# A decoder trunk's expert stage in two passes: gates scattered into a table in DRAM

## The chip, the cores and the metric

The kernel runs on one core of a Trainium2 chip. The metric is the time of one execution on the device in microseconds, the median of several. Matrix products run on TensorE, elementwise work and searches on VectorE (DVE in the profile), activations and casts on ScalarE (ACT), some elementwise work on GpSimd (POOL); SyncE (SP) issues most of the DMAs. The profile shows a matmul as PE and a weight load as PEld.

## The reference, cut to what matters

The program is a trunk of two layers on 256 tokens of width 1024. A layer is a mixing stage (a recurrence and attention side by side, one output projection, a layer norm) and then the expert stage, `_peer`. In it every token picks 128 of 16384 experts: 8 heads times 16.

```python
def _peer(x, wq, subkeys, u_tab, v_tab):
    xf = x.reshape(T, D)
    q = (xf @ wq).reshape(T, PEER_HEADS, 2, PEER_KEY_DIM)
    s = jnp.einsum('thcd,ckd->thck', q, subkeys).astype(jnp.float32)
    sv, si = lax.top_k(s, PEER_TOPK)
    cand = (sv[:, :, 0, :, None] + sv[:, :, 1, None, :]).reshape(T, PEER_HEADS, PEER_TOPK * PEER_TOPK)
    cv, ci = lax.top_k(cand, PEER_TOPK)
    ea = jnp.take_along_axis(si[:, :, 0], ci // PEER_TOPK, axis=-1)
    eb = jnp.take_along_axis(si[:, :, 1], ci % PEER_TOPK, axis=-1)
    experts = (ea * PEER_KEYS + eb).reshape(T, PEER_HEADS * PEER_TOPK)
    gate = jax.nn.softmax(cv, axis=-1).reshape(T, PEER_HEADS * PEER_TOPK).astype(x.dtype)
    ...
        act = jax.nn.gelu(jnp.einsum('cd,ced->ce', xc, u_tab[ec]))
        return jnp.einsum('ce,ced->cd', act * gc, v_tab[ec])
```

So the output of a token is a sum over its experts e of gate(e) * gelu(x . u[e]) * v[e]. Several heads of a token may pick the same expert; their gates then add up.

## The kernel before, in words

The kernel does not gather experts. It computes the dense form: for all 16384 experts and all 256 tokens the first product with gelu, multiplies it by a dense matrix G of gates (zero where an expert was not picked), and takes the second product with the whole of v. The experts are cut into 128 tiles of 128. Each tile has a first product (`u_tile`, lines 742 to 757) and a second one (`v_tile`, lines 977 to 985).

A first product is in one of two forms. In the split form (`wtile`, lines 97 to 109, and `col_mm` with `mm3`, lines 111 to 117) SyncE loads 512 KB into `raw` (four buffers), ScalarE casts it to `hi` (L104), VectorE or GpSimd subtracts to get `lo` (L105), and TensorE runs 8 x 3 matmuls (L113). In the f32 form (`raw_mm`, L140) TensorE multiplies the raw tile; the profile shows 16 records for its 8 matmuls. Tiles 14 to 33 have the f32 form, all others the split form; tiles 0 to 13 have their `lo` on GpSimd. Two tiles share a PSUM bank, and ScalarE's gelu (L752) writes a pair of them as one `act` tile of 256 KB.

A second product splits the weighted activations into W (ScalarE L963, VectorE L964), splits 512 KB of v in the same way, and runs 12 matmuls of 512 columns (L972) that sum up in four PSUM banks.

The order of a layer's expert stage is the program's text, lines 826 to 1086:
- queries and scores of the eight heads (`query`, `top`), each score row searched for its 16 largest on VectorE (`best16`, L791 to L795), the pair sums searched in the same way (`pairs`), with first products 0 to 13 behind them (lines 826 to 842);
- the choices: an exponential on ScalarE (L848), comparisons and sums in f16 on VectorE (L857 to L888), all eight heads at once;
- three transposes (L895), which give the experts' two halves and the gates by token (`eT`, `gT`);
- the one-hot stage: 32 rounds of `onehots` (lines 918 to 939), each two one-hot products on VectorE (L923, L927) for eight tokens, 16 matmuls (L934) and four copies on ScalarE (L938) into G, which fills 128 KB of every SBUF partition. Twelve f32 first products lie between the rounds;
- the dense stage (lines 1055 to 1081): first and second products alternate. The activations of the first 34 tiles, which were computed before G was there, had been written to DRAM (`kept`, issued by ScalarE) and are fetched back (`fetch`, L952); the others are used from SBUF. `w_pair` (L950) multiplies a pair by G.

Near the end of the stage parts of G are free and take weights of the next layer and the last tiles of v (`slot`, `take`, `parts`), and the last tiles are interleaved with the second layer norm by a hand-written order (`ORDER2`). The mixing stage has a hand-written order too, `ORDER`, one string of steps per layer; its steps `l0` to `l13` load w_out (`o0` to `o7`), the first queries' weights (`f0` to `f3`) and two tiles of wq (`w0`, `w1`). All these loads are on SyncE's queue, which runs in order and waits where a buffer is not free.

```python
for i in range(32):
    onehots(8 * i)
    while au < 2 * NSP and (au - 2 * NU0 + 1) * 32 <= (i + 1) * (2 * NSP - 2 * NU0):
        u_tile(au)
        au += 1
```

Of the kernel before, what the change touches and what calls it, by code (L numbers as in the profile page):

```python
# [21 lines left out]
S = 256  # L22
# [4 lines left out]
GSC = 32768.0  # L27

ORDER = ("d2 I0 c0 d4 I1 g2 d1 V3 c1 V1 V2 P V0 G3 G0 d0 G1 g0 b0 b1 g1 d3 T h0 d5 G2 q2 h1 q1 g3 kv D S q0 q3 "
# [19 lines left out]
NACT = 8  # L49
NU0 = 11  # L50
NSP = 17
# [18 lines left out]
for _name, _w in (("ident", 128), ("one", 1), ("av", 2), ("iota", 128), ("i16", 16), ("st16", 16), ("dist", 256),  # L70
                  ("ctab", 256), ("hm", 8), ("sel0", 128), ("sel1", 128)):
    CC[_name] = slice(_n, _n + _w)
    _n += _w
NCC = _n
NC0 = CC["av"].stop
# [3 lines left out]
def trunk_kernel(ctx: ExitStack, tc: tile.TileContext, x, xt, cst, lam, pvec, brow, w_in, w_lx, w_v, w_q4, lru_w,  # L79
# [162 lines left out]
    iota = cpool.tile([128, 128, 2], F16, name="iota")  # L242
# [21 lines left out]
    spill = ctx.enter_context(tc.tile_pool(name="spill", bufs=1, space=bass.MemoryType.DRAM))  # L264
    pw = {}
    nc.sync.dma_start(C, cst[:, :NC0])
    for l in range(NL):
# [3 lines left out]
        with tc.tile_pool(name="mix", bufs=1, reuse_waits="tile") as mp, \  # L271
# [7 lines left out]
            POOL.memset(onerow, 1.0)  # L279

# [377 lines left out]
            def tables():  # L658
                if l == 0:
                    softplus()  # L660
                    DVE.tensor_copy(identb, ident)
                    DVE.tensor_copy(iota, mc("iota").unsqueeze(2).to_broadcast([128, 128, 2]))
                    DVE.tensor_copy(i16[:, 0], mc("i16"))
                    DVE.tensor_copy(i16[:, 1], mc("st16"))
# [29 lines left out]
            def nsa_end(qb):  # L694
# [8 lines left out]
                         Q=qfirst, R=q_rows, I=lru_in, V=lru_conv, P=proj_v_end, d=const_load)  # L703
# [26 lines left out]
        with tc.tile_pool(name="peer", bufs=1, reuse_waits="tile") as pp:  # L730

            eT = pp.tile([128, 128, 2, 2], F16, name="eT")
            gT = pp.tile([128, 128, 2, 2], F16, name="gT")
            act = {}
            kept = {}

            ub = {}

            def act_tile():
                return pp.tile([128, 2, S], F32, name="act", bufs=NACT)  # L740

            def u_tile(a):
# [3 lines left out]
                if NPOOL <= a < 2 * NSP:  # L746
                    raw_mm(ps[:, HALF[a % 2]], rtile(u_tab[l, a], (8, 128)))
                else:
                    col_mm(ps[:, HALF[a % 2]], wtile(u_tab[l, a], (8, 128), POOL if a < NPOOL else DVE), xT)
                if a % 2:  # L750
                    at = act_tile()
                    ACT.activation(at.rearrange("p a b -> p (a b)"), ps, AF.Gelu_apprx_tanh)  # L752
                    if a // 2 < NSP:
                        kept[a - 1] = spill.tile([128, 2, S], F32, name="kept%d" % (a - 1), bufs=1)
                        ACT.dma_start(kept[a - 1], at)
                    else:
                        act[a - 1] = at

            def u_pair(a0):
                u_tile(a0)  # L760
                u_tile(a0 + 1)

            with tc.tile_pool(name="topk", bufs=1, reuse_waits="tile") as tk:
                skt = tk.tile([128, 2, 128], F32, name="skt")
                nc.sync.dma_start(skt, sk[l])
                sv = tk.tile([128, 2, 8, 2, 16], F32, name="sv")
# [3 lines left out]
                cd = tk.tile([128, 2, 8, NCAND], F32, name="cd")  # L770
                c2 = tk.tile([128, 2, 8, NCAND], F32, name="c2")
# [501 lines left out]
```

## Time and profile before

| | |
|---|---|
| median of 3 runs | 1962.98 us (1962.55 to 1965.69) |
| the profiled execution's own time | 1961.14 us |
| its span in the trace | 1959.4 us |
| mean granted clock of TensorE | 0.993 |
| TensorE busy | 1913.2 us, 98% |
| VectorE, ScalarE, GpSimd busy | 1285.2, 920.1, 126.0 us |
| read from HBM, written | 332.54 MB, 9.96 MB |

The busy shares are of the whole span. The layers are alike: mixing stage from 0 to about 154 us, expert stage to 976 us, then the second layer. Within the expert stage the rows below tell three stretches apart, the choices, the one-hots and the dense stage. A span's engine can be busy and still wait in the sense that its matmuls overlap in the pipeline, so prices of tiles are taken from the chain in order of time, where back-to-back work stands as one piece.

### The profile page before, as it was taken

To read this page: it belongs to the slowest core of one execution; us is meant where nothing else is said; L and a number is where in the kernel's file an instruction comes from. 1 tells how busy PE (TensorE), PEld (TensorE's weight loads), DVE (VectorE), ACT (ScalarE), POOL (GpSimd) and SP (SyncE) were. 2 spreads that over 40 slices of the span, in tenths; PEclk is the share of its full clock that TensorE was granted. 3 is DMA by queue.
4 is the path that set the end of the run, shared out by engine and by line. 5 is a ranking of instruction groups with operands and counts; after the bars stand their busy time and mean duration, and the time that the engine had idled before them with its cause. 6 is when DMAs were issued, how large, how long until landed. Compare 5 with 4: busy or idle time off the path is not lost.

```text
span 1959.4 us, 31424 instructions
## 1 busy us (share of the span) xinstructions
PE 1913.2 (98%) x12260; PEld 1676.5 (86%) x12260; DVE 1285.2 (66%) x2477; ACT 920.1 (47%) x1533; POOL 126.0 (6%) x71
## 2 busy tenths in 40 slices
PE   8999899999999999999999998999999999999998
PEld 7758898888888899999877488889888888999997
DVE  5756989565656555565567579896655665556555
ACT  3634425545454444454445344255545445445442
POOL 0005600000000000000000056000000000000000
PEclk9999899999999999999999999999999999999999
DMA  7405453666666666676362055436666676656552
GB/s 279 158 1 157 155 152 110 207 208 197 205 200 220 213 208 210 211 250 191 97 225 66 1 165 159 153 109 220 197 200 200 209 219 213 198 184 221 186 187 93
DMA packets 103017, 344.55 MB, mean 176 GB/s; under 512 B 12626, under 2 KB 13396, under 8 KB 102740
## 3 DMA queue, kind: packets, MB, share of 16 engines
q1 hardware_dynamic: 97972, 333.63, 53.6%
q10 hardware_dynamic: 4896, 8.92, 1.2%
q8 instruction: 96, 1.57, 0.3%
q14 instruction: 53, 0.43, 0.1%
HBM read 332.54 MB, written 9.96 MB: 175 GB/s over the span
## 4 chain that ended last, share of the span: by engine, by line
PE 87%; DVE 8%; DMA 2%; issue 2%; ACT 1%; POOL 1%; SPq 0%; DVEq 0%; POOLq 0%; ACTq 0%
PE ps L972 36%; PE ps L113 34%; PE ps L140 5%; PE ps L120 3%; PE ps L592 3%; DVE og L927 2%; DVE oh L923 2%; PE ps L934 2%; PE ps L564 1%; PE ps L517 1%; DMA raw<-in_wq_dram 1%; DVE si L795 1%; PE ps L233 1%; DVE s L793 1%; POOL lo L105 1%
## 5 line engine op out<-in xcount | busy, mean ns | idle before, releaser
L105 DVE TENSOR_TENSOR lo<-raw,hi 128x1024 fp32r<-128x1024 f32 x460 | 562.6, 1224 | 426.7 <-ACT hi L104 426.6
L104 ACT CAST hi<-raw 128x1024 fp32r<-128x1024 f32 x508 | 532.5, 1050 | 551.3 <-PE ps L113 321.0
L113 PE MATMUL ps<-xThi,hi 128*128 128x256 f32 x2080 | 594.2, 286 | 10.5 <-ACT hi L104 10.5
L113 PE MATMUL ps<-xThi,lo 128*128 128x256 f32 x2080 | 591.3, 284 | 5.9 <-POOL lo L105 5.1
L113 PE MATMUL ps<-xTlo,hi 128*128 128x256 f32 x2080 | 590.8, 284 | 0.0
L972 PE MATMUL ps<-hi,W 128*128 128x512 f32 x1936 | 550.5, 391 | 1.6 <-ACT W L963 1.6
L113 PEld LDWEIGHTS ps<-xThi,hi 128*128 128x128 f32 x2080 | 401.1, 193 | 18.8 <-ACT hi L104 10.9
L972 PEld LDWEIGHTS ps<-hi,W 128*128 128x128 f32 x1936 | 351.9, 189 | 65.8 <-ACT W L963 1.8
L113 PEld LDWEIGHTS ps<-xTlo,hi 128*128 128x128 f32 x2080 | 401.0, 193 | 7.3
L113 PEld LDWEIGHTS ps<-xThi,lo 128*128 128x128 f32 x2080 | 400.7, 193 | 6.6 <-POOL lo L105 5.7
L972 PE MATMUL ps<-lo,W 128*128 128x512 f32 x968 | 299.4, 390 | 0.0
L972 PEld LDWEIGHTS ps<-lo,W 128*128 128x128 f32 x968 | 181.8, 188 | 39.8
L963 ACT CAST W<-act 128x256 fp32r<-128x256 f32 x242 | 92.3, 405 | 145.9 <-PE ps L972 139.0
L140 PE MATMUL ps<-xTf,raw 128*128 128x256 f32 x704 | 158.1, 381 | 0.0
L140 PEld LDWEIGHTS ps<-xTf,raw 128*128 128x128 f32 x704 | 131.5, 190 | 17.6 <-issue 1.0
L105 POOL TENSOR_TENSOR lo<-raw,hi 128x1024 fp32r<-128x1024 f32 x48 | 122.5, 2566 | 329.6 <-ACT hi L104 329.5
L964 DVE TENSOR_TENSOR W<-act,W 128x256 fp32r<-128x256 f32 x242 | 97.3, 421 | 34.0 <-PE ps L972 31.5
L752 ACT ACTIVATE act<-ps 128x512 f32<-128x512 f32 x128 | 76.0, 593 | 92.8 <-PE ps L140 78.6
L950 DVE TENSOR_TENSOR act<-act,G 128x512 f32<-128x512 f32 x128 | 87.8, 686 | 44.5 <-DMA act<-kept 44.5
L938 ACT ACTIVATE G<-ps 128x256 f32<-128x256 f32 x256 | 74.8, 425 | 33.6 <-PE ps L934 31.9
L927 DVE TENSOR_TENSOR og<-oh,gT 128x2048 f16<-128x2048 f16 x64 | 76.0, 1219 | 0.7
L923 DVE TENSOR_TENSOR oh<-iota,eT 128x2048 f16<-128x2048 f16 x64 | 76.1, 1217 | 0.0
(256 smaller groups left out, 1293.0 us busy)
## 6 DMA issues: line engine op xcount, KB each, us to landing
raw<-in_u_tab_dram SPq DMA_DIRECT2D x256, 512.0 KB, 3.6
raw<-in_v_tab_dram SPq DMA_DIRECT2D x256, 512.0 KB, 3.6
raw<-in_w_in_dram SPq DMA_DIRECT2D x24, 512.0 KB, 4.5
raw<-in_wq_dram SPq DMA_DIRECT2D x24, 512.0 KB, 3.9
kept<-act ACTq DMA_DIRECT2D x34, 256.0 KB, 4.0
act<-kept SPq DMA_DIRECT2D x34, 256.0 KB, 4.3
ow<-in_w_out_dram SPq DMA_DIRECT2D x16, 512.0 KB, 7.4
qf<-in_w_q_dram SPq DMA_DIRECT2D x8, 512.0 KB, 3.8
```

The lines of the kernel that those rows point to most:

```text
L104: ACT.copy(hi, raw)
L105: lo_eng.tensor_tensor(lo, raw, hi, op=ALU.subtract)
L113: PE.matmul(ps, a[m], b[n], start=start and i == 0, stop=stop and i == 2)
L140: PE.matmul(ps, raw[:, c], xTf[:, c], start=c == 0, stop=c == NCH - 1)
L752: ACT.activation(at.rearrange("p a b -> p (a b)"), ps, AF.Gelu_apprx_tanh)
L923: DVE.tensor_tensor(oh.rearrange("p q w a i -> p (q w) a i"), iota.unsqueeze(1).to_broadcast([128, 8, 128, 2]), eT[:, qs].rearrange("p q w ...
L927: DVE.tensor_tensor(og, oh[:, :, 0:1].to_broadcast([128, 4, 2, 128, 2]), gT[:, qs].unsqueeze(3).to_broadcast([128, 4, 2, 128, 2]), op=ALU. ...
L938: ACT.activation(G[g][:, :, t1:t1 + 4], ps.rearrange("p (t g a) -> p g a t", g=2, a=64)[:, g], AF.Copy, scale=1.0 / GSC)
L950: DVE.tensor_tensor(act[a0], act[a0], G[a0 // 64][:, a0 % 64:a0 % 64 + 2, :], op=ALU.mult)
L963: ACT.copy(whi, at[:, a % 2])
L964: DVE.tensor_tensor(wlo, at[:, a % 2], whi, op=ALU.subtract)
L972: PE.matmul(accs[tb * 2 + hf], ww[m][:, TB[tb]], v[n][:, hf * 512:hf * 512 + 512], start=a == first[0] and (m, n) == (0, 0), stop=a == 127 ...
```

## The change

The gates no longer pass through one-hots. Each layer gets a table in DRAM of 128 x 128 x 256 f32 values (16.8 MB), one for every expert and token. In the mixing stage eight DMAs of 2 MB from a tile of zeros clear it; they are new steps `zt0` to `zt7` in `ORDER`, all on SyncE's queue: in layer 0 behind load `l3` and among `l4` to `l9`, in layer 1 from ahead of `l3` to ahead of `l8`. In the expert stage the eight heads are split into two groups of four. Once the choices of a group are known, the places are computed (expert * 256 + token) and GpSimd issues 128 indirect DMAs per group, each of which adds 128 gates, one per partition, to their places in the table (`scatter`). The DMAs go in batches of 16, one head and one half of the tokens each; a batch waits for the batch before it of the same token half.

All first products now come first, all in the split form, and their activations stay in SBUF in four quarters of 32 KB per partition. The steps of searching and choosing are generators that yield a number after each piece, and first products are placed between the pieces by these numbers, tile by tile. Queries of heads 4 to 7 are computed between the groups, with their `lo` on VectorE. Then all second products follow; each pair fetches its 256 KB of gates from the table (64 fetches per layer, three pairs ahead, the first behind a wait for the last scatters) and multiplies. `kept`, `eT`, `gT`, the transposes and the one-hots are gone. Buffers of activations go from 8 to 6 (`NACT`). The diff, cut:

```diff
+    table = [spill.tile([128 * 128 * S, 1], F32, name="table%d" % i) for i in range(NL)]
...
+            zeros = mpc.tile([128, 1024], F32, name="zeros")
+            POOL.memset(zeros, 0.0)
+
+            def clear(i):
+
+                n = 128 * 128 * S // 8
+                nc.sync.dma_start(table[l][i * n:i * n + n].rearrange("(p r k) o -> p r (k o)", p=128, k=1024),
+                                  zeros.unsqueeze(1).to_broadcast([128, n // 128 // 1024, 1024]))
...
-                if NPOOL <= a < 2 * NSP:
-                    raw_mm(ps[:, HALF[a % 2]], rtile(u_tab[l, a], (8, 128)))
-                else:
-                    col_mm(ps[:, HALF[a % 2]], wtile(u_tab[l, a], (8, 128), POOL if a < NPOOL else DVE), xT)
+                col_mm(ps[:, HALF[a % 2]], wtile(u_tab[l, a], (8, 128), POOL if a < NPOOL else DVE), xT)
                 if a % 2:
...
+                    ACT.activation(acts(a - 1).rearrange("p a b -> p (a b)"), ps, AF.Gelu_apprx_tanh)
...
-                                col_mm(ps[:, c * 256:c * 256 + 256], wtile(wq[l, k], (8, 128), POOL), xT)
+                                col_mm(ps[:, c * 256:c * 256 + 256], wtile(wq[l, k], (8, 128), POOL if h < 4 else DVE), xT)
...
+                            best16(sv[:, h // 4, j, c], si[:, h // 4, j, c], ss[:, k], s2[:, k])
+                            yield 1.45
...
+                def choices(g):
...
+                    DVE.scalar_tensor_tensor(ev[:, 0], ev[:, 0], 128.0, ev[:, 1], op0=ALU.mult, op1=ALU.add)
                     for tb in range(2):
...
+                        DVE.tensor_scalar(idx[:, g, j], ev[:, 0, j], float(S), C[:, CC["pt"]][:, tb:tb + 1],
+                                          op0=ALU.mult, op1=ALU.add)
+                    yield 0.7
+                    for h in range(4):
+                        for tb in range(2):
+                            scatter(g, h, tb)
+                    yield 0
+
+                def scatter(g, h, tb):
+
+
+                    j = tb * 4 + h
+                    before, sent[tb] = sent.get(tb, []), []
+                    for k in range(16):
+                        i = POOL.indirect_dma_start(table[l], bass.IndirectOffsetOnAxis(ap=idx[:, g, j, k:k + 1], axis=0),
+                                                    gate[:, g, j, k:k + 1], None, compute_op=ALU.add).ins
+                        tc.declare_no_dep(i, group="sent%d" % l, keep=before, reason="other places")
+                        wait_for(i, before)
+                        sent[tb].append(i)
...
+                def work():
+                    for h in (2, 0, 1, 3):
+                        yield from top(h)
+                    yield from pairs(0)
+                    yield from choices(0)
+                    for h in range(4, 8):
+                        query(h)
+                        yield 2.44 - 5.76
+                        yield from top(h)
+                    yield from pairs(1)
+                    yield from choices(1)
...
+                a, room = 0, 0.0
+                for cost in work():
+                    room -= cost
+                    while room < 0 and a < 96:
+                        u_tile(a)
+                        room += 2.88 if a < NPOOL else 1.66
+                        a += 1
...
+            for a in range(a, 128):
+                u_tile(a)
...
-                au = 2 * NU0
-                for i in range(32):
-                    onehots(8 * i)
...
                 def fetch(a0):
                     act[a0] = act_tile()
-                    nc.sync.dma_start(act[a0], kept[a0])
+                    i = nc.sync.dma_start(act[a0], table[l].rearrange("(a b t) o -> b a (t o)", b=128, t=S)[:, a0:a0 + 2])
+                    wait_for(i.ins, sent[0] + sent[1])
...
                 for j in range(2):
                     ready(j)
-                for _ in range(2):
-                    u_tile(todo.pop(0))
                 w_pair(body[0])
                 for j, p in enumerate(body):
                     ready(j + 2)
...
+                    ready(j + 3)
                     v_tile(p)
```

The pieces of `work` of one group yield 51 us in sum: 16 searches at 1.45, the pair sums with their eight searches at 2.4 and 8 x 1.05, and the choices at 17.

## Rows read from the trace of the kernel before

**Rows 1.** The page, engines: busy us, share of the span, instructions.

```profile
PE 1913.2 (98%) x12260; PEld 1676.5 (86%) x12260; DVE 1285.2 (66%) x2477; ACT 920.1 (47%) x1533; POOL 126.0 (6%) x71
```

**Rows 2.** The page, chain that ended last, shares of the span by line.

```profile
PE ps L972 36%; PE ps L113 34%; PE ps L140 5%; PE ps L120 3%; PE ps L592 3%; DVE og L927 2%; DVE oh L923 2%; PE ps L934 2%; PE ps L564 1%; PE ps L517 1%; DMA raw<-in_wq_dram 1%; DVE si L795 1%; PE ps L233 1%; DVE s L793 1%; POOL lo L105 1%
```

**Rows 3.** The chain in order of time: start us, us, what.

```profile
154.49 6.92 PE ps L140 x32
...
228.60 22.26 PE ps L113 x166
250.87 20.72 PE ps L140 x96
...
272.92 1.21 DVE oh L923
...
291.92 1.84 PE ps L934 x32
...
365.65 2.87 PE ps L113 x24
...
374.14 8.19 PE ps L972 x36
```

**Rows 4.** Windows: stretch, us, busy by engine, granted clock, DMA share, GB/s.

```profile
100.00:150.00 50.00, 48.61 (x191) 25.13 (x190) 28.14 (x98) 18.55 (x46) 0.00 (x0) 1.00 0.00 1
220.00:229.00 9.00, 1.34 (x6) 0.90 (x5) 8.93 (x39) 5.11 (x6) 3.72 (x2) 0.67 0.01 3
272.00:352.00 80.00, 78.80 (x738) 71.27 (x737) 76.91 (x70) 43.39 (x138) 0.00 (x0) 1.00 0.41 122
358.00:760.00 402.00, 400.44 (x2396) 357.93 (x2395) 241.99 (x287) 198.72 (x262) 0.00 (x0) 1.00 0.65 207
1330.00:1336.00 6.00, 6.00 (x48) 5.74 (x47) 2.36 (x4) 2.53 (x5) 0.00 (x0) 1.00 0.91 313
```

**Rows 5.** Groups of instructions: busy us, mean ns, idle before and its releasers.

```profile
L105 DVE TENSOR_TENSOR lo<-raw,hi 128x1024 fp32r<-128x1024 f32 x460 | 562.6, 1224 | 426.7 <-ACT hi L104 426.6
...
L964 DVE TENSOR_TENSOR W<-act,W 128x256 fp32r<-128x256 f32 x242 | 97.3, 421 | 34.0 <-PE ps L972 31.5 <-ACT W L963 1.3
...
L950 DVE TENSOR_TENSOR act<-act,G 128x512 f32<-128x512 f32 x128 | 87.8, 686 | 44.5 <-DMA act<-kept 44.5
L923 DVE TENSOR_TENSOR oh<-iota,eT 128x2048 f16<-128x2048 f16 x64 | 76.1, 1217 | 0.0
L927 DVE TENSOR_TENSOR og<-oh,gT 128x2048 f16<-128x2048 f16 x64 | 76.0, 1219 | 0.7
...
L878 DVE TENSOR_TENSOR t<-ge,dst 128x2048 f16<-128x2048 f16 x4 | 9.2, 2308 | 0.0
```

**Rows 6.** VectorE in order of time, first instruction of two searches in turn.

```profile
168.24 0.28 DVE L791 MAX8 sv<-ss 128x8 f32<-128x128 f32 x1
...
169.41 0.28 DVE L791 MAX8 sv<-ss 128x8 f32<-128x128 f32 x1
```

**Rows 7.** DMA queues (packets, MB, share of 16 engines) and issues (KB, us to landing).

```profile
q1 hardware_dynamic: 97972, 333.63, 53.6%
q10 hardware_dynamic: 4896, 8.92, 1.2%
...
out_dram<-xres SPq DMA_DIRECT2D x4, 256.0 KB, 2.2
```

**Rows 8.** SyncE's queue and TensorE in order of time, mixing stage of layer 0.

```profile
52.82 1.39 SPq L311 DMA_DIRECT2D ow<-in_w_out_dram  x3
...
124.11 1.98 PE L120 MATMUL ps<-qf,xTf 128*128 128x512 f32 x4
125.94 3.60 PE L592 MATMUL ps<-ow,yT 128*128 128x512 f32 x8
```

**Rows 9.** GpSimd's subtraction, 150 to 200 us and then 228 to 251 us.

```profile
L105 POOL TENSOR_TENSOR lo<-raw,hi 128x1024 fp32r<-128x1024 f32 x13 | 31.0, 2389 | 153.3 <-ACT hi L104 153.3
...
L105 POOL TENSOR_TENSOR lo<-raw,hi 128x1024 fp32r<-128x1024 f32 x7 | 20.7, 2982 | 10.3 <-ACT hi L104 10.3
```

More of the change, by code (lines that the diff above doesn't have):

```diff
@@ L69 @@
 _n = 0
[L70 removed]
+for _name, _w in (("ident", 128), ("one", 1), ("av", 2), ("pt", 2), ("i16", 16), ("st16", 16), ("dist", 256),
                   ("ctab", 256), ("hm", 8), ("sel0", 128), ("sel1", 128)):
@@ L826, in trunk_kernel @@
-                query(2)
-                q_rows(1)
-                query(0)
-                top(2)
-                query(1)
-                top(0)
-                query(3)
-                top(1)
-                for h in range(4, 8):
-                    query(h)
-                    top(h - 1)
-                    if h == 5:
-                        pairs(0, 4)
-                top(7)
-                for a in range(NPOOL):
-                    u_tile(a)
-                pairs(4, 8)
-                gt = tk.tile([128, 16, 16], F32, name="gt")
@@ L903, in trunk_kernel @@
-                for a0 in range(2 * NU0 - 2, 2 * NU0, 2):
-                    u_pair(a0)
-            with tc.tile_pool(name="dense", bufs=1, reuse_waits="tile") as dp:
-                G = [dp.tile([128, 64, S], F32, name="G", bufs=2) for _ in range(2)]
+                    yield 2.3
+                    DVE.tensor_tensor(t3, t3, sif[:, :, 1].unsqueeze(2).to_broadcast(shp), op=ALU.mult)
+                    yield 1.2
+                    tree(ev[:, 1], t3)
+                    DVE.tensor_reduce(gs, gt, axis=AX.X, op=ALU.add)
@@ new lines, in work @@
+                def work():
[9 more added lines that the diff above has]
+                    yield from choices(1)
+                for h in (2, 0, 1, 3):
+                    if h == 0:
+                        q_rows(1)
+                    query(h)
@@ L909, in trunk_kernel, with act_tile @@
+            def act_tile():
+                return dp2.tile([128, 2, S], F32, name="act", bufs=NACT)
+            if True:
                 more = l + 1 < NL
@@ L985, in v_tile @@
                         v_mm(a, ww, v, tb)
-                seq, k = [], 0
-                for i, f in enumerate(fresh):
-                    while k < NSP and k < 1 + (i + 1) * NSP / (0.55 * len(fresh)):
-                        seq.append(2 * k)
-                        k += 1
-                    seq.append(f)
+                seq = list(range(0, 128, 2))
                 tailp = list(range(nv, 128, 2))
@@ L998, in trunk_kernel @@
                 done = {q: max(place[4 * q], place[4 * q + 2]) for q in range(nv // 4)}
-                half = max(done[q] for q in range(16))
                 step = [0]
-                big = []
+                big, bigs = [], []
                 def take(n):
@@ L1010, in parts @@
                     if not big:
-                        assert step[0] >= half, (step, half)
-                        t = dp.tile([128, 16, 1024], F32R, tag="G", name="big", bufs=2)
-                        big.extend(t[:, i] for i in range(16))
+                        assert step[0] >= done[8 * len(bigs) + 7], (step, done)
+                        t = dp.tile([128, 8, 1024], F32R, tag="G", name="big", bufs=3)
+                        bigs.append(t)
+                        big.extend(t[:, i] for i in range(8))
                     return big.pop(0)
@@ L1042, in trunk_kernel @@
                       [(pre_wv, i) for i in range(3) if more]
-                todo = [a for p in seq if p >= 2 * NSP for a in (p, p + 1)]
-                def more_u(j):
-                    want = [p for p in seq[:j] if p >= 2 * NSP]
-                    n = 2 * (len(want) + 1)
-                    return n - (len(fresh) * 2 - len(todo))
                 def ready(j):
-                    if j < len(seq) and seq[j] in kept and seq[j] not in act:
+                    if j < len(seq) and seq[j] not in act:
                         fetch(seq[j])
@@ L1081, in trunk_kernel @@
                             f(i)
-                assert not pre and not todo, (pre, todo)
+                assert not pre, pre
                 gb = ln_gb(new_gb, (l, 2))
+                for j in range(len(body), len(seq)):
+                    ready(j)
                 for p in tailp[1:]:
```

183 lines of the change are left out of this document (70 added, 113 removed), and 8 rows, old and new, of the table ORDER.

## The prediction

> **What bounds the kernel now.** I read the engine shares first: TensorE is busy for 1913 of 1959.4 us, VectorE for 66% [rows 1]. The chain of waits then says where that time is: 36% in the second products (L972), 34% in the three-pass products (L113), 5% in the f32 first products (L140), and 5.6% in VectorE's one-hots and their matmuls (L923, L927, L934) [rows 2]. So a microsecond is won only where TensorE does less or stands still less. The chain in order of time gives the prices: a split tile of the first product (24 matmuls, L113) takes 2.87 us, an f32 tile (16 records of L140) 20.72 / 6 = 3.45 us, a second product (12 matmuls) 8.19 / 3 = 2.73 us, 32 one-hot matmuls 1.84 us [rows 3]. The windows show the two stretches of layer 0 where something else sets the pace: 220 to 229 us, where TensorE works for 1.34 us of 9 at a granted clock of 0.67, and the one-hot stage, where VectorE is busy for 76.9 of 80 us [rows 4]. Layer 1 has the same two.
>
> **What goes, per layer.** (1) The one-hot stage: 32 rounds of one L923 and one L927, 1.217 + 1.219 us each [rows 5], are 78.0 us of VectorE. TensorE does 12 f32 tiles in it, 12 x 3.45 = 41.4 us, which return elsewhere. Gone: 36.6 us. The one-hot matmuls (512 x 0.0575 = 29 us) lie inside that. (2) All 20 f32 tiles become split tiles: 20 x (3.45 - 2.87) = 11.6 us gained. Their splits cost 20 x 1.22 us more on VectorE [rows 5] and as many casts on ScalarE, beside TensorE. (3) The stall at 220: 9 - 1.34 = 7.7 us, and the 166 matmuls after it took 22.26 us instead of 166 x 0.12 = 19.9, the rate of the full-clock tile; the clock was the lower of its two levels, 1.2 GHz, for part of it, after TensorE had stood still. Together 10 us. It came from ScalarE's exponential, which waits behind VectorE's backlog of top-16 searches. After the change every second or third step of that work has a first-product tile beside it, so I count the stall as gone. (4) The three transposes and copies between the last f32 tile of that stretch (250.87 + 20.72) and the first one-hot at 272.92 us [rows 3]: 1.3 us. Sum 59.5 us per layer, 119 us in all.
>
> Costed at nothing: the 17 writes of activations per layer that ScalarE's queue no longer issues, and the clearing of 128x1024 zeros on GpSimd, which is idle at that place; the eight query tiles whose subtraction goes from GpSimd to VectorE (8 x 1.22 us), which the change allots beside 5.76 us of TensorE per head. If VectorE were behind there, those 9.8 us would show on TensorE.
>
> **What comes.** The top-16 work itself is the same. A 128-wide search runs at 1.17 us [rows 6], where the change allots 1.45 us, so VectorE should not fall behind its cover; the exponential now comes twice, and I keep 3 us for it (0 to the old 10).
>
> **The clears** write 16.8 MB per layer from SyncE's queue, amid the weight loads of the mixing stage. The only writes of before, on q10, took 1.2% x 16 x 1959.4 us for 8.92 MB, so 23.7 GB/s per engine or 379 GB/s [rows 7]: 44 us. The ten loads of 0.5 MB behind or between them (four of w_out, four of w_q, two of wq) need 5.2 MB at q1's 333.63 MB / (0.536 x 1959.4 us) = 318 GB/s, 16 us. SyncE reaches them at about 53 us, so all has landed at 113; the first w_q matmul is at 124.1 and the w_out rows that wait for the last pieces at 125.9 [rows 8]. DMA stands at 0.00 from 100 to 150 us [rows 4], which is the cover. At the highest rate of any row, 313 GB/s [rows 4], it is 70 us and 123; at the 207 GB/s of the dense stage, 22 MB need 106 us, until 159, 35 us late. I take 3 us, with 0 and 35 as ends.
>
> **The gates read back** are 64 fetches of 256 KB per layer instead of 17. In the second pass a pair of tiles takes 5.46 us and needs 1.31 MB: 240 GB/s, under the 313 seen. VectorE then needs 2 x (1.22 + 0.42) + 0.69 = 3.97 us per pair [rows 5], also under 5.46. Both hide behind TensorE; without that cover the fetch alone would be up to 5.3 us a pair. They are issued three pairs ahead, but the first stands on SyncE's queue behind all scatters, and every weight load of the second pass stands behind it. Passing from one pass to the other costs a landing, a product and a split, 6 us at most; part of it lies under the last buffered tiles, so 4 us.
>
> **The scatters** decide. Each layer issues 256 indirect DMAs from GpSimd, one at a time on its queue: 2 groups x 8 batches x 16. Let p be the time of one. Count from the first query matmul (154.5 us [rows 3]). Four queries take 6.9 + 5.75 us of TensorE. Group 0 carries 51 us of allotted VectorE time, met by 14 tiles at 2.88 and 6.5 at 1.66, so 20.5 x 2.87 = 59 us: its scatters start at +72. Group 1's start some 95 us later. The first pass ends at 6.9 + 10 x 2.87 + 128 x 2.87 = +403; the first gates must be on their way 6 us earlier, at +397. That leaves 325 us for 256: they are hidden while **p is under 1.27 us**. The gain of 59.5 - 10 = 49.5 us is used up at (325 + 50) / 256 = **1.46 us**.
>
> The trace has no indirect DMA. Below lies the issue of a plain load on SyncE's queue, 1.39 us for three, 0.46 each [rows 8]: 118 us, hidden. Above lies a write that is waited for until it lands, 2.2 us [rows 7]: 563 us, 238 late. Their geometric middle is 1.0. A GpSimd instruction that reads SBUF stretches beside VectorE work with two inputs: the same subtraction took 2.39 us beside the searches and 2.98 beside the 2.3 us f16 products of L872 to L884 [rows 5, 9], 25% more. That makes 1.25 us, just under the limit. I take it: hidden, at 0 us, with 238 us per layer as the other end.
>
> Each scatter also puts 128 additions of 4 bytes on the 16 DMA engines. Nothing that small is priced in the rows; above lies q10's mean packet, 1.2% x 16 x 1959.4 us / 4896 = 77 ns for 1.8 KB [rows 7], so 256 x 8 x 0.077 = 158 us of each engine per layer, below lies nothing. The weight loads of the pass need 128 x 0.524 MB / 318 GB/s = 211 us; 369 in all fit into 397 even at the upper end, so I take no delay, though at that end single tiles would be late.
>
> The Trainium skill speaks against the change here: SBUF — State Buffer, "Who interferes with whom", says that a GpSimd instruction that reads SBUF and a VectorE instruction with two SBUF inputs block each other outright, whoever comes second. The rows above agree that there is contention, but show 0.59 us on an instruction beside 2.3 us products, not a full wait. The Trainium skill's DMA: Bandwidth & Descriptors ("Latency and other measured facts") puts the first byte of a DMA from GpSimd at about 1 us; an estimate by that alone is 256 us per layer, hidden.
>
> Adds per layer: 3 + 3 + 4 + 0 = 10 us; net 49.5, twice 99. The profiled execution had 1961.1 us (span 1959.4), so 1862; the median of the runs shown, 1963.0, lies 1.9 above it: **1864 us**.
>
> **Rivals.** (A) *GpSimd's queue becomes the bound.* From p = 1.46 us on, the kernel is slower than before: SyncE's first fetch waits for the last scatter, all second-product loads stand behind it, and TensorE idles between the passes. At 1.75 us: 448 - 325 = 123 late per layer, 1864 + 246 = 2110 us; at 2.2: 2340. For it: every step of this is in order on one queue, the limit is close, and searching and scattering start late. Against it: nothing else is on GpSimd then, and 16 scatters run between one batch and the batch that must wait for it. (B) *Late, but not that late:* p between 1.27 and 1.44, at 1.36 (348 - 325) x 2 = 46 us, 1910. (C) *The clears crowd the weight loads:* 35 us per layer less 3, 1928 us. For it the 0.5 MB loads that sit between them; against it the idle 50 us. (D) *The change trades one cost for an equal one,* p near 1.46: within 0.2% of 1963. (E) *The shared port blocks in full:* with L105 on VectorE for 1.22 of every 2.87 us, only one scatter fits in each gap of 1.65; 256 x 2.87 = 735 us, 410 late per layer, 2684 us. It is the rule of the Trainium skill's SBUF — State Buffer above. Rows 9 bear it out only in part.
>
> **How the numbers follow.** Forecast 0.47, A 0.30, B 0.11, C 0.05, D 0.03, E 0.04. 0.2% is about what a measurement of this kernel can tell from no change. Faster: 0.47 + 0.11 + 0.05 = 0.63; same 0.03; slower 0.34. The forecast alone reaches from 1838 (nothing added, 1963 - 119, and 3 us per layer of other stalls gone) to 1890 (all three adds at about twice their size and a few late tiles). The range must take in B, C, D and the nearer half of A, up to p = 1.72 (115 late per layer): 1838 to 2095. Out of it are E, the rest of A (about 0.12) and little below.
>
> **What the profile after would show.** Right: no stretch after 220 us with TensorE idle; a first pass of 24-matmul tiles at 2.87 us without breaks, then blocks of 12 at 2.73; indirect DMAs on GpSimd that end before the last first-product tile; the last w_out load landed before the row products want it. Wrong: SyncE waiting on GpSimd's DMAs at the first fetch, a gap of TensorE between the passes, and a clock at its lower level after it (A, B, E); the w_out or w_q products waiting for DMA (C); first-product tiles apart by more than 2.87 us while scatters run, because 4-byte writes fill the 16 engines. If the passes meet without a gap and the time still falls less than 60 us, a term of the sum is wrong, and the stall of part 3 is the first to look at.

## The result and the profile after

The change takes 2461.98 us (median of 4 runs, 2460.97 to 2465.27) against 1964.12 us for the kernel before: **1.2538 times the time, 95% interval 1.2516 to 1.2559**, 498 us more. The prediction was 1864 us, range 1838 to 2095.

The page of the kernel after: engines, four of the rows in 40 slices, the queue of GpSimd's DMAs, the chain by line, and the group of scatters.

```profile
PE 1845.4 (75%) x11544; PEld 1615.8 (66%) x11544; DVE 1166.8 (47%) x2428; ACT 901.9 (37%) x1323; POOL 1007.2 (41%) x569
...
PE   9999999990000499999999999999900004999998
...
POOL 0024667778888300000000346788888882000000
PEclk9999999995555699999999999999955557999999
...
GB/s 298 325 77 159 154 188 185 183 172 0 0 0 0 137 222 251 234 263 266 178 234 273 98 160 147 197 181 183 152 0 0 0 0 146 231 235 247 236 262 132
...
q0 software_dynamic: 73728, 0.29, 8.2%
...
POOL table L901 25%; PE ps L974 18%; DMA table<-gate,idx 16%; PE ps L110 10%; DMA act<-table 5%; PE ps L117 2%; PE ps L598 2%; DVE lo L102 1%; DMA raw<-in_v_tab_dram 1%; DVE W L966 1%; PE ps L230 1%; DMA acts<-in_lnrow_dram 1%; PE ps L570 1
...
L901 POOL DMA_INDIRECT table<-gate,idx x512 | 923.0, 1803 | 286.2 <-DMA table<-gate,idx 124.7
```

TensorE's work fell from 1913 us [rows 1] to 1845. The time went to two stretches of four slices each where TensorE and the loads both stand and GpSimd alone works. The chain is led by the scatters (L901, 25%) and their landings (16%), where the second products led before [rows 2]. Windows of layer 0 (columns as in [rows 4]: busy us and count of PE, PEld, VectorE, ScalarE and GpSimd, then granted clock, DMA share, GB/s): the choices of the first group, scatters beside first products, the stop, the rest of the first pass, the second pass.

```profile
163.00:240.00 77.00, 73.05 (x563) 71.70 (x562) 53.98 (x236) 37.21 (x47) 39.47 (x16) 0.96 0.52 170
240.00:552.00 312.00, 308.25 (x2561) 307.13 (x2561) 170.16 (x339) 140.86 (x165) 223.25 (x110) 1.00 0.68 178
560.00:833.00 273.00, 0.00 (x0) 0.00 (x0) 2.12 (x3) 1.41 (x5) 221.55 (x143) 0.50 0.24 7
833.00:864.00 31.00, 30.54 (x237) 30.54 (x238) 18.65 (x22) 13.82 (x17) 0.00 (x0) 0.92 0.71 229
864.00:1230.00 366.00, 356.25 (x1549) 287.66 (x1548) 242.76 (x336) 187.63 (x265) 1.37 (x7) 1.00 0.73 236
```

110 scatters run in the 312 us beside the first products, 143 in the 273 us of the stop. With TensorE still, the granted clock is at its lower level, 1.2 GHz (0.50). Who waits, over the whole kernel (engine, line, releaser: us in total, times, longest):

```profile
DVE act L951 <- DMA act<-table: 736.4, 105, 280.4
PEld ps L110 <- DVE lo L102: 557.1, 7, 279.0
...
SPq L955 <- DMA table<-gate,idx: 562.8, 8, 277.5
```

SyncE's queue stands at the first fetch (L955) until the last scatter has landed; VectorE stands at the first gate product (L951). Behind each stand the loads and subtractions of the last first-product tiles, so TensorE waits in the *first* product (L110), not in the second. The chain in order of time shows how it ends:

```profile
823.43 3.00 DMA table<-gate,idx
827.47 4.08 DMA act<-table
833.46 30.84 PE ps L110 x238
864.30 5.92 PE ps L974 x26
```

238 matmuls, ten tiles of 24, were still to do. Last, the price of a scatter. GpSimd in order of time, alone in layer 0 and then beside tiles in layer 1 (start, us, and in brackets the idle time before):

```profile
804.83 1.56 POOL L901 DMA_INDIRECT table<-gate,idx  x1 [0.30 <-issue]
806.70 1.55 POOL L901 DMA_INDIRECT table<-gate,idx  x1 [0.31 <-issue]
...
1683.89 2.57 POOL L901 DMA_INDIRECT table<-gate,idx  x1 [0.30 <-issue]
1686.77 2.56 POOL L901 DMA_INDIRECT table<-gate,idx  x1 [0.30 <-issue]
```

and VectorE in the second stretch:

```profile
1683.81 1.23 DVE L102 TENSOR_TENSOR lo<-raw,hi 128x1024 fp32r<-128x1024 f32 x1 [1.65 <-ACT hi L101]
1686.69 1.23 DVE L102 TENSOR_TENSOR lo<-raw,hi 128x1024 fp32r<-128x1024 f32 x1 [1.65 <-ACT hi L101]
```

Alone a scatter takes 1.55 us, 1.86 from one to the next. Beside a subtraction of 1.23 us it takes 1.02 more, and each tile lets one through: the scatter ends 2.65 us after the subtraction's start (1686.46), the next starts 0.30 later, and by then the next subtraction has begun (1686.69).

In layer 0 the same pace of one scatter a tile is made in another way. Two scatters and the subtractions that they met, and GpSimd's wait for landings from 240 to 552 us:

```profile
340.40 1.55 POOL L901 DMA_INDIRECT table<-gate,idx  x1 [1.56 <-DMA table<-gate,idx]
401.41 2.18 POOL L901 DMA_INDIRECT table<-gate,idx  x1 [0.69 <-DMA table<-gate,idx]
...
340.46 1.23 DVE L102 TENSOR_TENSOR lo<-raw,hi 128x1024 fp32r<-128x1024 f32 x1 [1.65 <-ACT hi L101]
400.94 1.23 DVE L102 TENSOR_TENSOR lo<-raw,hi 128x1024 fp32r<-128x1024 f32 x1 [1.66 <-ACT hi L101]
...
POOL table L901 <- DMA table<-gate,idx: 78.6, 79, 3.1
```

79 of the 110 scatters there wait for an earlier one to land, 78.6 us in sum, and take 2.03 us on average. The order of the starts decides what a subtraction costs. Over both layers 16 scatters started ahead of the subtraction that they met, with VectorE idle at that moment (as at 340.40): they took 1.54 to 1.56 us, and the subtraction 1.22 or 1.23. Of 168 that started within a subtraction, 163 took longer by what was left of it, less 0.12 us (0.76 of it left at 401.41, 0.63 longer). VectorE loses next to nothing either way.

### The profile page after: what moved, and what is told of

It is laid out like the page before. It is cut to its first block, busy times and chain, and to the rows that moved or that the text cites. A ratio compares the mean times of both kernels' runs of the same rounds, so it can differ in the third digit from the quotient of the medians.

```text
span 2459.2 us, 30413 instructions
## 1 busy us (share of the span) xinstructions
PE 1845.4 (75%) x11544; PEld 1615.8 (66%) x11544; DVE 1166.8 (47%) x2428; ACT 901.9 (37%) x1323; POOL 1007.2 (41%) x569
## 3 DMA queue, kind: packets, MB, share of 16 engines
q0 software_dynamic: 73728, 0.29, 8.2%
## 4 chain that ended last, share of the span: by engine, by line
PE 38%; POOL 26%; DMA 24%; issue 8%; DVE 3%; ACT 1%; SPq 0%; DVEq 0%; POOLq 0%; ACTq 0%
POOL table L901 25%; PE ps L974 18%; DMA table<-gate,idx 16%; PE ps L110 10%; DMA act<-table 5%; PE ps L117 2%; PE ps L598 2%; DVE lo L102 1%; DMA raw<-in_v_tab_dram 1%; DVE W L966 1%; PE ps L230 1%; DMA acts<-in_lnrow_dram 1%; PE ps L570 1%; PE ps L523 1%; PE ps L137 1%
## 5 line engine op out<-in xcount | busy, mean ns | idle before, releaser
L110 PE MATMUL ps<-xThi,lo 128*128 128x256 f32 x2400 | 685.6, 286 | 561.6 <-DVE lo L102 555.8
L901 POOL DMA_INDIRECT table<-gate,idx x512 | 923.0, 1803 | 286.2 <-DMA table<-gate,idx 124.7
L110 PEld LDWEIGHTS ps<-xThi,lo 128*128 128x128 f32 x2400 | 465.8, 194 | 563.5 <-DVE lo L102 557.1
L102 DVE TENSOR_TENSOR lo<-raw,hi 128x1024 fp32r<-128x1024 f32 x516 | 629.7, 1221 | 332.9 <-ACT hi L101 332.3
L110 PE MATMUL ps<-xThi,hi 128*128 128x256 f32 x2400 | 687.9, 287 | 2.1 <-ACT hi L101 2.1
L110 PE MATMUL ps<-xTlo,hi 128*128 128x256 f32 x2400 | 684.0, 285 | 0.0
L110 PEld LDWEIGHTS ps<-xThi,hi 128*128 128x128 f32 x2400 | 465.8, 194 | 3.4 <-ACT hi L101 2.5
L110 PEld LDWEIGHTS ps<-xTlo,hi 128*128 128x128 f32 x2400 | 465.8, 194 | 0.3
L951 DVE TENSOR_TENSOR act<-act,acts 128x512 f32<-128x512 f32 x128 | 88.3, 692 | 736.4 <-DMA act<-table 736.4
L753 ACT ACTIVATE acts<-ps 128x512 f32<-128x512 f32 x128 | 75.8, 592 | 0.1
L793 DVE MAX8 sv<-ss 128x8 f32<-128x128 f32 x64 | 16.8, 283 | 60.0 <-ACT ss L808 57.8
```

The lines of the kernel that those rows point to most:

```text
L102: lo_eng.tensor_tensor(lo, raw, hi, op=ALU.subtract)
L110: PE.matmul(ps, a[m], b[n], start=start and i == 0, stop=stop and i == 2)
L753: ACT.activation(acts(a - 1).rearrange("p a b -> p (a b)"), ps, AF.Gelu_apprx_tanh)
L901: i = POOL.indirect_dma_start(table[l], bass.IndirectOffsetOnAxis(ap=idx[:, g, j, k:k + 1], axis=0), gate[:, g, j, k:k + 1], None, compute ...
L951: DVE.tensor_tensor(act[a0], act[a0], acts(a0), op=ALU.mult)
```

## The experiments

Theory: the scatters' price on GpSimd's queue sets when the second pass may start; 2.87 us while VectorE reads two inputs, 1.86 otherwise. Rivals: landings and loads on the DMA engines; the order on the queues; a cost per scatter wherever it stands. Each is one run, beside a run of the kernel before on the same chip; these took 1962.0 to 1965.6 us.

### No scatters

```
-                    for k in range(16):
+                    for k in range(0):
```

> The changed kernel with its 512 indirect DMAs left out (the gates are then all zero); clears, fetches and both passes stay. Theory S (the scatters alone cost the time): about 1875 us, that is 1964 less the 99 of the prediction and some 10 more for the clears of layer 0, with no gap of TensorE between the passes. Rival R (other parts of the change cost too, the fetches or the clears): over 1920 us.

Measured: 1908.84 us. So the scatters cost 553 us, and the rest gains 54 (1963.08 on the same chip) instead of the predicted 99. Windows of layer 0, the stretch that the prediction counted as gone and the second pass, and one row of the waits:

```profile
215.00:230.00 15.00, 8.85 (x54) 8.44 (x54) 14.93 (x52) 6.18 (x8) 3.31 (x1) 0.77 0.18 56
...
590.00:957.00 367.00, 356.73 (x1546) 287.40 (x1545) 242.31 (x336) 187.56 (x265) 1.48 (x7) 1.00 0.72 235
```

```profile
DVE act L951 <- DMA act<-table: 182.3, 105, 4.4
```

TensorE still stands 6 of 15 us while VectorE is busy for all but 0.07 of them, and the second pass takes 367 us where 128 blocks at 2.73 us [rows 3] are 349. Neither theory had this number; two runs below take it apart.

### First products without VectorE

```
-                col_mm(ps[:, HALF[a % 2]], wtile(u_tab[l, a], (8, 128), POOL if a < NPOOL else DVE), xT)
+                if a < NPOOL:
+                    col_mm(ps[:, HALF[a % 2]], wtile(u_tab[l, a], (8, 128), POOL), xT)
+                else:
+                    raw_mm(ps[:, HALF[a % 2]], rtile(u_tab[l, a], (8, 128)))
```

> First products 14 to 127 in the f32 form, so that VectorE has no two-input subtraction beside the scatters while the 512 KB loads go on (3.45 us a tile instead of 2.87). Theory L (the shared port: a scatter stands still while VectorE runs a two-input instruction): 1.86 us from scatter to scatter beside the tiles too, as it is now only after them; the scatters of a layer end some 100 us sooner and the kernel takes about 2260 us. Rival M (the weight loads on the DMA engines delay them): still 2.6 us or more beside the tiles, and 2460 us or more.

Measured: 2513.76 us. GpSimd beside the tiles:

```profile
341.80 1.55 POOL L904 DMA_INDIRECT table<-gate,idx  x1 [1.08 <-DMA table<-gate,idx]
343.65 1.57 POOL L904 DMA_INDIRECT table<-gate,idx  x1 [0.30 <-issue]
345.75 1.56 POOL L904 DMA_INDIRECT table<-gate,idx  x1 [0.53 <-DMA table<-gate,idx]
```

A scatter takes 1.55 us again. The edit takes out ScalarE's casts too; but in the change itself 11 scatters met a cast and no subtraction, and took 1.54 to 1.58 us, so the stretch is VectorE's. Waits for landings remain, and the mean from one to the next is 2.30 us (340 to 540 us), not the 1.86 of theory L. The total missed theory L's 2260 us and lies in rival M's range. The chain shows why it says little:

```profile
771.68 3.08 DMA table<-gate,idx
...
781.87 95.39 PE ps L137 x432
```

432 matmul records, 27 f32 tiles, stood behind the wait for the last scatter, 95 us in layer 0.

### First products without loads

```
+                    raw = xTf[:, 0:4].rearrange("p a b -> p (a b)")   (tiles 14 to 127)
```

> First products 14 to 127 keep ScalarE's cast and VectorE's subtraction but take a tile that lies in SBUF, so their loads of u are left out (the products are those of other data). Theory L (shared port): 2.87 us from scatter to scatter beside the tiles as before, within 1% of 2462 us. Rival M (weight loads): 1.86 us, and about 2260 us.

Measured: 2446.37 us, within 1% of the change. GpSimd:

```profile
344.41 2.57 POOL L908 DMA_INDIRECT table<-gate,idx  x1 [0.30 <-issue]
347.28 2.57 POOL L908 DMA_INDIRECT table<-gate,idx  x1 [0.30 <-issue]
```

The same 2.87 us without a wait for a landing between them (in the whole run these waits fall from 124.7 to 17.1 us). So VectorE's subtraction is enough for this pace, and to take the traffic away wins next to nothing. It does not follow that the traffic alone would let scatters through faster than the change does; the last two experiments come back to that.

### First products ahead of the wait

```
+                    behind(i.ins, ulast["dve"])      (first gate products, behind the last subtraction)
...
+                    behind(i.ins, ulast["sp"])       (fetches, behind the last load of the first pass)
```

> The changed kernel with the first products' last loads and subtractions kept ahead of the first fetch and the first multiplication by the gates on SyncE's and VectorE's queues. Theory Q (ten tiles of the first pass stand behind the wait, since their instructions are queued behind it): those 29 us per layer move into the wait, the ten scatters beside them take 1 us more each, so 19 us less per layer, about 2424 us. Rival: the order is not what holds them, and the time stays at 2462 us.

Measured: 2433.21 us, 14.4 us a layer less (19 were expected): the ten tiles moved out of the way. The stop itself stays.

### Half of the scatters

```
-                    for k in range(16):
+                    for k in range(0, 16, 2):
```

> Leaves out every second scatter (the odd picks of each head and token half), so 128 instead of 256 indirect DMAs a layer; half of the gates are missing from the output. Theory L (a scatter costs 2.87 us beside the subtractions and 1.86 us alone, and only what does not fit beside the first products costs time): in layer 0 the scatters begin at 240.6 us, 109 of the 128 fit until TensorE stops at 552 us, the other 19 at 1.86 us end at 588 us, the gates are there at about 596 us, the ten tiles behind the wait take 31 us, and the second products begin at about 627 us where the kernel without scatters begins them at 590 us. That is 37 us a layer over it, 1909 + 74 = about 1983 us. Rival N (each scatter slows the kernel by the same amount wherever it stands, 553 us over 512 scatters = 1.08 us): 1909 + 256 x 1.08 = 2185 us.

Measured: 2173.12 us, within 12 us of the rival. The windows say why:

```profile
420.00:540.00 120.00, 0.00 (x0) 0.00 (x0) 0.00 (x0) 0.00 (x0) 99.84 (x65) 0.51 0.24 0
540.00:717.00 177.00, 171.30 (x1405) 171.30 (x1406) 80.05 (x73) 78.89 (x94) 0.00 (x0) 0.97 0.60 193
```

TensorE stood already at 420 us, with 1405 matmuls, 58 tiles, of the first pass queued behind the wait. With fewer scatters ahead of it, the wait had been put earlier on the queues, and half the scatters still stopped TensorE for 120 us. So this run did not tell the theories apart until the order was fixed.

### Half, and a quarter, with the order fixed

The edits of the last two runs together; for a quarter, `range(0, 16, 4)`.

> Every second scatter left out (half of the gates missing from the output), and the order of the run e4: the last loads and subtractions of the first pass stand ahead of the first fetch on SP's queue and of the first gate product on VectorE. The run with half of the scatters had 58 first-product tiles queued behind the wait and TensorE still from 417 to 546 us. Theory Q+L (the order on the queues cost that run its time; what is left is a scatter of 2.87 us beside a subtraction): from 240.6 us on about 122 scatters fit until the first products end at 590 us, the last 6 at 1.86 us end at 601 us, the gates are there at 609 us, some 20 us a layer behind the kernel without scatters: 1909 + 40 = about 1949 us. Rival N (each scatter takes its 1.08 us from the kernel wherever it stands): 2173 to 2185 us again.

> Three of four scatters left out (three quarters of the gates missing from the output), in the same order. Theory Q+L: 64 scatters at 2.87 us last 184 us and end at about 425 us, 165 us ahead of the last first product, so that they are hidden in full: the time of the kernel without scatters, 1909 us, or up to 10 us more for transfers and VectorE's own lock. Rival N: 1909 + 128 x 1.08 = 2047 us.

Measured: 1953.98 and 1905.32 us, 5 and 4 us from the theory, 142 or more from the rival. The windows of the run with half:

```profile
240.00:590.00 350.00, 341.22 (x2834) 339.91 (x2833) 181.25 (x346) 152.90 (x179) 266.06 (x125) 1.00 0.65 171
590.00:610.00 20.00, 0.71 (x2) 0.61 (x3) 3.58 (x6) 2.59 (x6) 6.01 (x4) 0.50 0.60 175
```

64 scatters cost nothing. Of 128, 125 fit beside 350 us of first products, and a gap of some 20 us a layer remains: the last three, their landing and the first fetch. What does not fit costs its 1.86 us alone.

### Half of the places in each scatter

```
-  ... bass.IndirectOffsetOnAxis(ap=idx[:, g, j, k:k + 1], axis=0), gate[:, g, j, k:k + 1] ...
+  ... bass.IndirectOffsetOnAxis(ap=idx[:64, g, j, k:k + 1], axis=0), gate[:64, g, j, k:k + 1] ...
```

> Every scatter sends the picks of the first 64 partitions only (as many indirect DMAs as in the change, half the places in each; half of the gates are missing from the output). Theory D (the 1.55 us of a scatter go by the number of places that GpSimd writes descriptors for): a scatter takes about 0.8 us and 1.1 us to the next when it stands alone; beside the tiles one or two fit in each gap between the subtractions, so that all 256 end at the latest about where the first products do, and the kernel takes between 1909 and 2050 us. Rival F (a fixed price for each indirect DMA): 1.55 us again, 1.86 us to the next, and 2462 us.

Measured: 2392.3 us. GpSimd, alone:

```profile
704.01 1.39 POOL L901 DMA_INDIRECT table<-gate,idx  x1 [0.30 <-issue]
705.71 1.40 POOL L901 DMA_INDIRECT table<-gate,idx  x1 [0.30 <-issue]
```

64 places less save 0.15 of 1.55 us: nearly all of the price is fixed (rival F; 512 x 0.15 = 77 us is about what the run lies under its 2462).

### No fetches, and no clears

```
-                    DVE.tensor_tensor(act[a0], act[a0], acts(a0), op=ALU.mult)
+                    DVE.tensor_tensor(act[a0], acts(a0), acts(a0), op=ALU.mult)   (and no dma_start in fetch)
```

For the second run also `clear(i)` without its DMA.

> Leaves out the scatters and also the fetches of the gates: the second pass multiplies the first products by themselves in place of the fetched gates. Beside the kernel without scatters (1908.84 us, second products in 367 us and 357 us where 1536 matmuls at 227 ns make 349 us). Theory F (the fetches on SP's queue, each waiting for a buffer of the split before it, hold the second pass back): the second passes take 349 to 352 us and the time is 1908.8 - 18 - 8 = about 1883 us. Rival B (the second pass is bound by the loads of its own weights or by the splits on VectorE): 1905 to 1909 us.

> Leaves out the scatters, the fetches and the clears of the tables. Theory C (the clears crowd the mixing stages: the first query copy comes 8.9 us later in layer 0 than in the kernel before, and 4.8 us later after the second products in layer 1): 13 to 14 us less than the kernel without scatters and fetches. Rival O (what is late in the mixing stages is late for the order of the work, not for the clears): no change from it.

Measured: 1880.81 and 1872.51 us. The fetches cost 28 us, as expected by F; that it is their waiting for buffers, as F says, this run does not show. One line of the second products in layer 0 (count, ns, first and last start), without scatters and then also without fetches:

```profile
L974 PE MATMUL ps<-hi,W x960: 387/389/398, 589.8 to 933.3; 128*128 128x512 f32 x192
```

```profile
L972 PE MATMUL ps<-hi,W x960: 387/389/501, 584.9 to 915.1; 128*128 128x512 f32 x192
```

343.5 us become 330.2. The clears cost 8.3 us, less than the 13 to 14 of theory C; the rest of what is late in the mixing stages is not theirs.

### The fetches on ScalarE's queue

```
-                    i = nc.sync.dma_start(act[a0], table[l]...
+                    i = ACT.dma_start(act[a0], table[l]...
```

> The kernel without scatters, with the fetches issued from ScalarE's queue in place of SP's. Without the fetches it took 28 us less (1880.8 against 1908.8 us; second passes of 353 and 350 us against 367 and 357 us). Theory SPQ (a fetch that waits for its buffer holds up the loads behind it on SP's queue, and the other way round): about 1885 to 1890 us. Rival LAT (the gates arrive late because of the ring of six buffers and the 3.6 to 5 us that a fetch takes to land, whichever queue issues it): 1905 to 1915 us. ScalarE's own stream may also be held up by a fetch that waits: over 1915 us then.

Measured: 1990.78 us, the last case: a new wait of ScalarE in the second pass of layer 0, where it stands for VectorE's split to free a buffer:

```profile
ACT W L965 <- DVE W L966: 149.8, 43, 5.4
```

So this other queue is no cure; more buffers were not tried.

### One input in place of two

```
-  lo_eng.tensor_tensor(lo, raw, hi, op=ALU.subtract)
+  DVE.tensor_scalar(lo, raw, 0.0, None, op0=ALU.mult)      (first-product tiles 14 to 127, order as above)
```

> The run e4 (all scatters, first products ahead of the wait), but on VectorE the low half of first-product tiles 14 to 127 is the weight times zero, an instruction with one input, in place of the weight minus its high half, with two: the low halves are left out of these products. Theory T (it is the second SBUF input that stops GpSimd): the scatters beside the tiles take 1.55 us again; at 1.86 us from one to the next some 188 of the 256 fit into the 350 us beside the first products in place of 122, at the 2.30 us of the run with f32 tiles, where landings were waited for, 152. At 1.86 us each that is 30 to 66 scatters, 56 to 123 us a layer, less: 2433 - 112 to 246 = 2187 to 2321 us. Rival V (any VectorE instruction of this size stops GpSimd, with one input too): scatters between 2.0 and 2.6 us beside the tiles and a time over 2380 us.

Measured: 2394.82 us, the time of rival V; the scatters lie between the two. GpSimd and VectorE beside the tiles of layer 0:

```profile
401.58 1.82 POOL L908 DMA_INDIRECT table<-gate,idx  x1 [1.06 <-DMA table<-gate,idx]
404.33 1.97 POOL L908 DMA_INDIRECT table<-gate,idx  x1 [0.93 <-DMA table<-gate,idx]
...
401.29 0.69 DVE L108 TENSOR_SCALAR lo<-raw 128x1024 fp32r<-128x1024 f32 x1 [2.18 <-PE ps L117]
```

The one-input instruction is shorter (0.69 us) and still stretches the scatter that starts within it, so theory T is not confirmed: one input stops GpSimd too in this form. And where the stop got shorter, a wait for landings filled the tile: 2.85 us on average from 300 to 580 us. In layer 1 it is 2.49.

### More room for descriptors

```
-dynamic_dma_scratch_size=1024
+dynamic_dma_scratch_size=4096
```

on the run with one input, and on the run with the order alone.

> The run e13 (low halves of first-product tiles 14 to 127 left out, one-input instruction in their place) with 4096 in place of 1024 bytes a partition for the descriptors of GpSimd's DMAs. In e13 a scatter beside the tiles took 1.82 us but the next came after 2.87 us in layer 0, about 1 us of it waiting for an earlier scatter to land. Theory R (that wait is for room for descriptors): it goes, scatters come every 2.1 to 2.2 us beside the tiles, some 162 of 256 fit into 350 us in place of 122, 74 us a layer less than e4's 2433 us: 2270 to 2300 us. Rival B (the wait is for something else, the landing of additions behind 0.5 MB loads in the DMA queues whatever the room): within 15 us of e13's 2395 us.

> The run e4 (nothing left out, first products ahead of the wait) with 4096 in place of 1024 bytes a partition for descriptors. Theory L (beside the subtractions GpSimd's stop sets the pace, one scatter a tile, and the waits for landings lie under it, as in the run without loads): 2433 us within 10. Rival R' (the room for descriptors sets the pace in the change itself): 2270 to 2400 us.

Measured: 2345.72 and 2426.91 us. With one input the waits shrink (2.2 to 2.5 us from one scatter to the next in layer 0; layer 1 hardly changed), 49 us in all, half of what R expected: room is a part of that wait, and what the rest is stays open. In the kernel with the real subtraction it is worth 6 us, hardly more than the chips differ by (theory L), though waits for landings stay there too: 65 of 126 scatters in layer 0, 59.9 us.

So there are two bounds, and in layer 0 both lie near one scatter a tile: without the loads the stop holds the pace (2.87 us), and with a shorter stop the landings hold it (2.85). Where both are eased it falls only part of the way, to 2.49 in layer 1 of the run with one input, 2.35 in layer 0 with more room, and 2.30 without subtractions and with the slower f32 tiles.

## Why the prediction was wrong

**The step that failed: the price of a scatter, taken as p = 1.25 us and so "hidden, at 0 us".** Measured: 1.86 us alone, over the limit of 1.27 and over the break-even of 1.46, so by the prediction's own sum the change had to lose even without contention: 256 x 1.86 = 476 us where 325 were to be had. Neither of the two rows around it priced the thing at issue, the time that GpSimd itself spends on one indirect DMA, and so the middle between them was no estimate.

**The contention was read too mildly.** The 25% came from [rows 9], where GpSimd ran a subtraction of its own beside two-input work of VectorE that hardly paused, and where both sides lost:

```profile
229.00:251.00 22.00, 22.00 (x168) 21.97 (x168) 22.00 (x14) 5.88 (x8) 16.94 (x6) 0.90 0.66 215
...
229.55 3.40 DVE L878 TENSOR_TENSOR t<-ge,dst 128x2048 f16<-128x2048 f16 x1
```

VectorE is busy for all 22 us, and L878 takes 3.40 us where the mean is 2.31 [rows 5]. A scatter shares otherwise: beside a subtraction that is under way it takes 2.57 us instead of 1.55, and the subtraction keeps its 1.23. That is rival E's mechanism, given 0.04, and E's 2.87 us from one scatter to the next is the measured one, in layer 0 with waits for landings as a part of it. The mechanism is also the rule of the Trainium skill's SBUF — State Buffer ("Who interferes with whom"). The trace agrees with it for a scatter that comes second; a subtraction that comes second is not held up (1.23 us at 340.46, 0.06 us after a scatter's start), and there the measurement decides.

E's 2684 us was too much because it let the stop last for all 256 scatters: it ends when the first products stop, and the rest run at 1.86 us. A's path was right in every step (SyncE's fetch, loads behind it, TensorE idle, clock at the lower level), its prices of 1.75 to 2.2 us too low for the mean of 2.29. The result lies between them, at 110 scatters of 2.87 and 146 of 1.86 us a layer: 587 us for 325, 262 late per layer, 1864 + 524 = 2388; the two paragraphs below add 29 and 45 us, and that makes 2462.

**A step that was missing: what else stands behind the wait.** The prediction put the second pass's loads there. Ten tiles of the first pass stood there as well, 14 us a layer (58 tiles in the run with half of the scatters, where it decided, and 27 in the run with f32 tiles).

**Gains and small costs, by the run without scatters: 54 us instead of 99.** The fetches, costed at nothing since 240 GB/s is under the 313 seen, cost 28: the second pass waits for them although the rate is 235 GB/s; whether that is for the six buffers, the order on the queue or the DMA engines' load was not told apart. The stall of part 3, counted as gone with 10 us, is there again beside the first tiles, and ScalarE's exponential waits for VectorE again:

```profile
219.22 0.31 ACT L842 ACTIVATE gate<-gate 128x128 f32<-128x128 f32 x1 [7.80 <-DVE gate L841]
```

In layer 0 of that run 54 matmuls took 15 us at a clock of 0.77, where 54 x 0.12 are 6.5, so 8.5 are lost; in layer 1, from 1168 to 1184 us, 79 took 16, so 6.5. The clears took 8.3 us in all against 2 x 3. The passage from one pass to the other, set at 4 us, does not show; in the chain one follows the other:

```profile
573.98 15.96 PE ps L110 x133
589.94 15.21 PE ps L974 x67
```

The sum had 20 us of such costs, 2 x (3 for the exponential, where the stall is, + 3 + 4). Measured are 28 + 15 + 8 = 51. That explains 31 of the 45 us that are missing; the other 14 stay open, and which of the gains (one-hot stage, f32 tiles, transposes) came as counted was not measured singly. **Right:** the 4-byte additions on the DMA engines. 8.2% x 16 x 2459 us / 73728 packets is 44 ns each, under the upper end of 77, and the first products beside them keep their pace: TensorE is busy for 308 of 312 us.

**Could it win?** With 256 scatters a layer, no version seen here does: the kernels with the order fixed and nothing left out take 2427 and 2433 us, and even at 1.86 us throughout, 476 us of scatters are 126 more than the 350 beside the first products, over the gain of 27 us a layer. With 128 it takes 1954 us against 1965 before, but that leaves out half of the gates. Fewer DMAs with several places for each partition were not tried, nor scatters started ahead of each subtraction.

## What to carry to other kernels

Before work is moved to a queue that was idle, find the price of one such instruction on that engine by itself, and multiply: here the issuing engine alone needed 476 us a layer for 256 small DMAs. Price it again beside the busiest neighbour: beside the tiles it was 1.5 times as much. Where a pace seems explained by one cause, take that cause away and look whether another holds it: here the stop and the waits for landings each did. And where a wait is added, list everything that the order has put behind it on that queue, earlier work too: how much that is can change with the wait's own length, and can hide what an experiment is meant to show.

## What was not expected of the hardware

An indirect DMA of 128 places of 4 bytes holds GpSimd for 1.55 us and one of 64 places for 1.40. What a VectorE instruction costs it depends on which starts first: a scatter that starts ahead of the subtraction keeps its 1.55 us, one that starts within it waits for the rest. A VectorE instruction with one input (128x1024, f32, 0.69 us) stretched the scatters beside it too, to 1.8 to 2.0 us. And scatters wait for earlier ones to land, 0.7 us each in layer 0 of the change, with 1024 bytes of descriptors a partition; with 4096 they are as long there (59.9 us against 57.7 with the order fixed, 240 to 590 us).
